# Attention with plain fp32 products in place of split ones, output by tokens, one PSUM pool, and the first two channel tiles interleaved

## The chip, the cores and the metric

The kernel runs on one core of a Trainium2 chip. A core has five engines with instruction streams of their own: TensorE (matmul and transpose, PE in the views, its weight loads PEld), VectorE (DVE), ScalarE (ACT), GpSimd (POOL) and SyncE (SP), which here issues most of the transfers. TensorE's results land in PSUM, eight banks of 128 x 512 fp32. The metric is the time of one execution in device microseconds; the times given are medians of several runs. One further execution was recorded by the hardware profiler. Its own time is given beside its span, since all rows below belong to it.

## The reference

One decoder layer over 512 tokens and 1024 channels, all in fp32: a SwiGLU FFN (inner width 2816), a mixing stage, a second FFN, each behind an RMSNorm and with a residual. The change is in the mixing stage:

```python
h = rms_norm(x, mix_norm_w[l])
z, xbc, dt_raw, q, k, v = jnp.split(h @ w_in[l], split_idx, axis=-1)
xbc = jax.nn.silu(causal_dwconv(xbc, conv_w[l], conv_b[l]))
...
y_ssd = ssd_chunked(xs, dt, a, bm, cm, d_skip[l])      # chunks of 128 tokens, 16 heads of 64
q = rms_norm(q.reshape(bsz, s, ATT_HEADS, 2, ATT_QK_DIM), q_norm_w[l])   # 8 heads, 2 halves of 64
k = rms_norm(k.reshape(bsz, s, ATT_HEADS, 2, ATT_QK_DIM), k_norm_w[l])
...
sc = jnp.einsum("bqhtd,bkhtd->bhtqk", qi, kf) * scale
p = jax.nn.softmax(jnp.where(mask, sc, -jnp.inf), axis=-1)
att = p[:, :, 0] - lam * p[:, :, 1]
o = jnp.einsum("bhqk,bkhd->bqhd", att, vf)             # v: 128 wide per head
o = rms_norm(o, attn_subln_w[l]) * (1.0 - lambda_init)
x = x + jnp.concatenate([y_ssd, o], axis=-1) @ w_out[l]
```

So each of 8 heads has two score matrices, and their softmaxes are subtracted before the product with v; the head's output is normed over its 128 channels.

## The kernel before, in words

Every large product is made of three matmuls in F32R, a single-pass type with fewer bits: an operand is split into a high part (the cast) and a low part (what the cast left), and hi·hi, hi·lo and lo·hi are summed in PSUM (`mm3`, L168 to L172; `tok_proj`, L590, with its matmuls in L603 to L605). Weights arrive by SyncE's transfers in pieces of 128 x 1024 (`raw`), `split_part` makes `whi` (ScalarE's cast in L128, or GpSimd in L126 while `pool_hi` is set) and `wlo` (VectorE's subtraction in L129). `piece()` asks for pieces two ahead. fp32 matmuls without a split exist beside them, such as cb (L644) and the transposes; the profile records a true fp32 product as two instructions.

The order within each engine is made by a scheduler from the program's text, with a simulated timeline; buffers and banks that come free, and true dependences, are its limits.

In time the stages are: FFN1 (0 to about 357 us), whose results are added to x by L362 channel tile by channel tile, each followed by the norm's scaling and split (`xh` L236, `xl` L237); the mixing stage; FFN2 (from about 843). The mixing stage is:

- Channel projections (L562 to L583): six pairs of 128-channel tiles, each tile 8 x 3 matmuls of 512 columns over `nm.xh`, `nm.xl`, weights stationary. `pA` gives two banks for a pair. The first pair also lets the norm finish (`finish`, L249: row sums into psr, the rsqrt chain of VectorE, psb). `conv_tile` (L470 to L488) does convolution and SiLU, `conv_tr` (L490) transposes by xt, `dt_proj` (L498 to L516) makes psdt and its transposes psdtT.
- SSD: z and v projections by tokens (`z_group`, `v_group`, L613 to L632) run between the chunks' work: `ssd_a` (L636: decay ab by Relu and Exp on ScalarE, its product with cb on VectorE, y), `ssd_o` and `ssd_d` (state, pd). v is stored split (`vhl`, L431).
- Attention (L966 to L998): the projections qk of heads 1 to 7 and parts of the head output wo serve as fillers (`fill`, L938) between the steps of a head. `qk_half` (L769) forms q and k and splits them (qs, kh, kl), `qk_tr` (L803) transposes them by 24 matmuls a head, `att_s` (L821) makes the scores of a 128-query block, masks, takes the maximum, the exponentials and the combination of the two softmaxes in pe; `att_t` (L848) transposes pe and splits it into atH and atL; `att_av` (L861) multiplies by v with channels on the partitions; `att_n` (L876) norms with a matmul with ones (om); `o_split` (L910) splits the result for wo. GpSimd takes part in nearly all of these.

PSUM is handed out by pools that are closed and opened again between stages (`psum_open`, L49): eight banks of one kind for FFN1, then A=2 (two banks each), M=2, J=2 (L424), then J=2, M=4, A=1 for attention, then eight again. A tile of a new pool waits for whoever reads the old pool's tile in the same place.

## Time and profile before

| what | value |
|---|---|
| median of 3 runs | 1196.5 us (1195.9 to 1197.11) |
| profiled execution | 1194.4 us, its span 1192.3 |
| mean granted TensorE clock | 0.992 |
| TensorE busy | 1160.0 us, 97% of the span |
| VectorE, ScalarE, GpSimd busy | 895.1, 569.6, 155.2 us |

The span is what the rows of the trace cover. A record's length is not the time that an instruction holds the engine: TensorE's records overlap by about 0.17 us, so the distance between two starts is the better measure. In the groups of instructions the part behind the bar gives the busy sum, the mean of one record in ns, and the idle time of the engine just before them with what ended it.

### The profile page before, as it was taken

Reading aid. Unit: us, or ns where it says so; the run is one execution under the profiler, and the core shown is the slowest. Engines: PE = TensorE matmul, PEld = TensorE weight load, DVE = VectorE, ACT = ScalarE, POOL = GpSimd, SP = SyncE. Lnnn points to the kernel's source line nnn. Section 1 sums busy time; section 2 is a strip of 40 time slices with the busy share of each in tenths; the row PEclk is TensorE's granted clock in tenths of the full one; section 3 lists DMA queues with packets and bytes.
Section 4 is the critical chain, followed back from the end, with each engine's and each line's share of the span. In section 5 each row is a group of like instructions: output and inputs, shape, how many; then the busy total and the mean of one; then the engine's idle time right before and its main releaser. Section 6 shows DMA issues by size and latency. Waiting matters only on the chain.

```text
span 1192.3 us, 18991 instructions
## 1 busy us (share of the span) xinstructions
PE 1160.0 (97%) x7483; PEld 1033.1 (87%) x7483; DVE 895.1 (75%) x1485; ACT 569.6 (48%) x991; POOL 155.2 (13%) x178
## 2 busy tenths in 40 slices
PE   8999999999998999999999998899999999999998
PEld 6889999999986788999988896688789999999997
DVE  6988787887675875976588988636599888787863
ACT  5433443343353448973366766735244444343331
POOL 1000000000022000000346656423000000000000
PEclk9999999999998999999999999999999999999999
DMA  6223333233253223423221103025213333333232
GB/s 231 89 76 98 100 108 99 92 111 106 89 186 127 77 90 107 142 89 110 88 70 48 60 19 124 27 63 211 80 62 105 108 111 98 110 107 102 96 108 84
DMA packets 42393, 119.56 MB, mean 100 GB/s; under 512 B 4608, under 2 KB 9920, under 8 KB 42304
## 3 DMA queue, kind: packets, MB, share of 16 engines
q1 hardware_dynamic: 41024, 114.15, 29.8%
q0 software_dynamic: 1280, 4.20, 1.0%
q8 instruction: 59, 0.97, 0.3%
q14 instruction: 30, 0.25, 0.1%
HBM read 112.00 MB, written 6.32 MB: 99 GB/s over the span
## 4 chain that ended last, share of the span: by engine, by line
PE 83%; DVE 8%; ACT 4%; issue 2%; POOL 1%; DMA 1%; SPq 0%; ACTq 0%; POOLq 0%; DVEq 0%
PE s L327 9%; PE s L326 9%; PE s L328 9%; PE dn L170 6%; PE dn L172 6%; PE dn L171 6%; PE gu L170 3%; PE gu L172 3%; PE gu L171 3%; PE wo L172 2%; PE wo L170 2%; PE wo L171 2%; PE xbc L170 2%; PE xbc L171 2%; PE xbc L172 2%
## 5 line engine op out<-in xcount | busy, mean ns | idle before, releaser
L128 ACT CAST whi<-raw 128x1024 fp32r<-128x1024 f32 (+2 forms) x204 | 176.6, 868 | 309.5 <-PE s L327 121.7
L129 DVE TENSOR_TENSOR wlo<-raw,whi 128x1024 fp32r<-128x1024 f32 (+3 forms) x225 | 226.5, 1010 | 113.4 <-ACT whi L128 102.0
L327 PE MATMUL s<-al,whi 128*128 128x256 f32 x952 | 265.0, 279 | 0.0
L326 PE MATMUL s<-ah,whi 128*128 128x256 f32 x952 | 263.4, 279 | 0.0
L328 PE MATMUL s<-ah,wlo 128*128 128x256 f32 x952 | 262.4, 279 | 0.0
L327 PEld LDWEIGHTS s<-al,whi 128*128 128x128 f32 x952 | 178.7, 188 | 2.1
L326 PEld LDWEIGHTS s<-ah,whi 128*128 128x128 f32 x952 | 178.3, 188 | 2.0
L328 PEld LDWEIGHTS s<-ah,wlo 128*128 128x128 f32 x952 | 177.1, 187 | 0.1
L128 ACT CAST whi<-tw 128x1024 fp32r<-128x1024 f32 x68 | 70.4, 1051 | 141.0 <-PE s L327 65.6
L170 PE MATMUL dn<-h,whi 128*128 128x512 f32 x352 | 137.5, 394 | 0.0
L172 PE MATMUL dn<-h,wlo 128*128 128x512 f32 x352 | 137.5, 392 | 0.0
L171 PE MATMUL dn<-h,whi 128*128 128x512 f32 x352 | 136.8, 389 | 0.0
L129 DVE TENSOR_TENSOR wlo<-tw,whi 128x1024 fp32r<-128x1024 f32 x68 | 82.0, 1220 | 2.9 <-ACT whi L128 2.8
L172 PEld LDWEIGHTS dn<-h,wlo 128*128 128x128 f32 x352 | 66.1, 188 | 14.6
L171 PEld LDWEIGHTS dn<-h,whi 128*128 128x128 f32 x352 | 66.1, 188 | 12.7
L170 PEld LDWEIGHTS dn<-h,whi 128*128 128x128 f32 x352 | 66.1, 188 | 12.2
L603 PE MATMUL qk<-whi,xhm 128*128 128x256 f32 x256 | 74.1, 289 | 0.3 <-DVE kf L781 0.3
L605 PE MATMUL qk<-whi,xlm 128*128 128x256 f32 x256 | 73.4, 287 | 0.0
L604 PE MATMUL qk<-wlo,xhm 128*128 128x256 f32 x256 | 73.1, 286 | 0.0
L362 DVE SCALAR_TENSOR_TENSOR x<-dn,x 128x512 f32<-128x512 f32 x64 | 44.1, 688 | 35.3 <-PE dn L172 34.8
L170 PE MATMUL gu<-xh,whi 128*128 128x512 f32 x160 | 65.0, 406 | 3.4 <-POOL whi L126 2.3
L172 PE MATMUL gu<-xh,wlo 128*128 128x512 f32 x160 | 63.7, 398 | 0.0
(293 smaller groups left out, 2529.1 us busy)
## 6 DMA issues: line engine op xcount, KB each, us to landing
raw<-in_gu SPq DMA_DIRECT2D x86, 512.0 KB, 3.5
raw<-in_dn SPq DMA_DIRECT2D x48, 384.0 KB, 3.1
raw<-in_wqk SPq DMA_DIRECT2D x16, 512.0 KB, 3.7
raw<-in_wxbc SPq DMA_DIRECT2D x12, 512.0 KB, 3.6
raw<-in_wo SPq DMA_DIRECT2D x10, 512.0 KB, 4.4
raw<-in_dn SPq DMA_DIRECT2D x16, 256.0 KB, 2.6
raw<-in_wz SPq DMA_DIRECT2D x8, 512.0 KB, 3.5
raw<-in_wv SPq DMA_DIRECT2D x8, 512.0 KB, 3.6
```

Of the source, the lines that this page charges most:

```text
L128: S.copy(hi[:, a:b], raw[:, a:b])
L129: V.tensor_sub(lo[:, a:b], raw[:, a:b], hi[:, a:b].bitcast(F32))
L170: PE.matmul(ps, lhsT=hi, rhs=xh, start=start, stop=False)
L171: PE.matmul(ps, lhsT=hi, rhs=xl, start=False, stop=False)
L172: PE.matmul(ps, lhsT=lo, rhs=xh, start=False, stop=stop)
L326: PE.matmul(ps, lhsT=hi, rhs=ah[:, i, a], start=i == 0, stop=False)
L327: PE.matmul(ps, lhsT=hi, rhs=al[:, i, a], start=False, stop=False)
L328: PE.matmul(ps, lhsT=lo, rhs=ah[:, i, a], start=False, stop=i == 3)
L362: V.scalar_tensor_tensor(x[d], ps, 0.5, x[d], op0=ALU.mult, op1=ALU.add)
L603: PE.matmul(o, lhsT=xh, rhs=hi, start=k == 0, stop=False)
L604: PE.matmul(o, lhsT=xh, rhs=lo, start=False, stop=False)
L605: PE.matmul(o, lhsT=xl, rhs=hi, start=False, stop=k == KD - 1)
```

## The change

PSUM becomes a single pool of eight one-bank tiles for the whole kernel; `pM`, `pJ` and `pP` are the same. In the first pair of channel tiles the loop over k is outside: for each k three matmuls of one tile and three of the other, into two banks; `finish` starts behind both, and the pair's convolution is issued behind the first tile of the second pair. v is kept in fp32 (`vt`).

In attention q and k stay fp32, 128 channels (both halves) to a row of tokens, so 8 fp32 transposes a head take the place of 24. The scores of half t use rows 64t to 64t+63 of the transposed q and k as a contraction over 64, one fp32 matmul for each half and query block, K columns long, into two banks. The combination of the softmaxes isn't divided by the first sum any more: pe0 − lam·(l0/l1)·pe1 is used, and the norm's epsilon is multiplied by l0² instead. The product with v is made by tokens: 10 fp32 matmuls of 128 x 128 a head; the norm is done there with a free-axis reduction, and `att_o` transposes the result (4 a head) and splits it. GpSimd has no part in it: weights' high parts and y's copy are ScalarE's. The order of steps in the loop over heads is changed. The diff, shortened:

```diff
--- before.py
+++ after.py
@@ -44,31 +44,12 @@
-    psum = {}
-    def psum_open(**bufs):
...
-    def pA(name):
-        return psum["A"][1].tile([P, 2, T], F32, tag="A", name=name)
+    pspool = ctx.enter_context(tc.tile_pool(name="psum", bufs=8, space=PSUM))
     def pM(name, dt=F32):
-        return psum["M"][1].tile([P, T], dt, tag="M", name=name)
-    def pJ(name):
-        return psum["J"][1].tile([P, T], F32, tag="J", name=name)
...
-    def pP(name):
-        return psum["P"][1].tile([P, T], F32, tag="P", name=name)
+        return pspool.tile([P, T], dt, tag="P", name=name)
+    pJ = pP = pM
...
@@ -421,16 +401,16 @@
-    psum_open(A=2, M=2, J=2)
...
-    vhl = [[mix.tile([P, NB, 256], F32R, tag=f"v{z}{g}", name=f"v{z}{g}") for z in "hl"] for g in range(4)]
+    vt = [mix.tile([P, NB, 256], F32, tag=f"v{g}", name=f"v{g}") for g in range(4)]
...
@@ -565,21 +545,30 @@
-        ps = pA(f"xbc{n}")
+        ps = [pP(f"xbc{n}{i}") for i in range(2)]
+        if n == 0:
+            ws = [piece(), piece()]
+            for k in range(KD):
+                for p_, w in zip(ps, ws):
+                    mm3(p_, w, k, nm.xh[:, k, :], nm.xl[:, k, :], k == 0, k == KD - 1)
+            fin = nm.finish()
+            next(fin)
+            first_ps = ps
+            continue
         for i in range(2):
             w = piece()
             for k in range(KD):
-                mm3(ps[:, i, :], w, k, nm.xh[:, k, :], nm.xl[:, k, :], k == 0, k == KD - 1)
-            if n == 0 and i == 0:
-                fin = nm.finish()
+                mm3(ps[i], w, k, nm.xh[:, k, :], nm.xl[:, k, :], k == 0, k == KD - 1)
+            if n == 1 and i == 0:
                 next(fin)
-            elif n == 0:
-                next(fin)
+                pend0 = [(t, conv_tile(t, p_)) for t, p_ in zip(order[0], first_ps)]
         if n == 3:
             dt_finish(pt_dt)
         for t, dst in pend:
             conv_tr(t, dst)
-        pend = [(t, conv_tile(t, ps[:, i, :])) for i, t in enumerate(pair)]
+        pend = [(t, conv_tile(t, ps[i])) for i, t in enumerate(pair)]
+        if n == 1:
+            pend = pend0 + pend
...
-                h, lo = (z[:, j, :] for z in vhl[g])
-                S.activation(h, ps[:, jj, :], AF.Copy, scale=nm.r[:, j:j + 1])
-                V.scalar_tensor_tensor(lo, ps[:, jj, :], nm.r[:, j:j + 1],
-                                       h.bitcast(F32), op0=ALU.mult, op1=ALU.subtract)
+                S.activation(vt[g][:, j, :], ps[:, jj, :], AF.Copy, scale=nm.r[:, j:j + 1])
...
@@ -667,11 +653,11 @@
-        pd = pds[c, g] = pA(f"pd{c}{g}")
+        pd = pds[c, g] = [pP(f"pd{c}{g}{i}") for i in range(2)[:2 if c else 1]]
         if c > 0:
-            PE.matmul(pd[:, 1, :], lhsT=cT[:, g, cs], rhs=state[:, g, :], start=True, stop=True)
+            PE.matmul(pd[1], lhsT=cT[:, g, cs], rhs=state[:, g, :], start=True, stop=True)
...
@@ -775,22 +761,12 @@
...
-        qf = at.tile([P, 2, P], F32, tag="qf", name="qf")
+        qf = at.tile([P, 2, P], F32, tag="qf", name="qf", bufs=4)
         V.tensor_tensor(qf, ps[:, :, 0:P], wqk_row.unsqueeze(1).to_broadcast([P, 2, P]), op=ALU.mult)
...
+        kf = at.tile([P, 2, P], F32, tag="kf", name="kf", bufs=4)
+        V.tensor_tensor(kf.rearrange("p a (b c) -> p a b c", c=64), ps[:, :, P:].rearrange("p a (b c) -> p a b c", c=64),
                         rs[:, :, 2:4].unsqueeze(3).to_broadcast([P, 2, 2, 64]), op=ALU.mult)
...
-        qk[h].append((rs, qs, kh, kl))
+        qk[h].append((rs, qf, kf))
     qk = {}
@@ -802,92 +778,91 @@
     def qk_tr(h):
         res = []
+        for si, tag in enumerate(("qT", "kT")):
+            pt = pM(f"{tag}{h}")
+            for j in range(NB):
+                PE.transpose(blk(pt, j), qk[h][j // 2][1 + si][:, j % 2, :], ident)
+            d = at.tile([P, T], F32, tag=tag, name=tag, bufs=2)
+            S.copy(d, pt)
+            res.append(d)
+        qkT[h] = res
+    ls, sm, aT = {}, {}, {}
+    def att_s(h, i):
+        K = (i + 1) * P
+        if i == 0:
+            ls[h] = tiny.tile([P, 2, NB], F32, tag="l", name="l", bufs=3)
+        ps = [pM(f"sc{h}{i}{t}") for t in range(2)]
+        qT, kT = qkT[h]
         for t in range(2):
...
-    def att_s(h, i):
-        K = (i + 1) * P
-        kc = max(K, 256)
...
+            r = slice(t * 64, t * 64 + 64)
+            PE.matmul(ps[t][:, :K], lhsT=qT[r, i * P:K], rhs=kT[r, :K], start=True, stop=False)
         for t in range(2):
-            qT, khT, klT = qkT[h][3 * t:3 * t + 3]
-            PE.matmul(ps[:, t, :kc], lhsT=blk(qT, i), rhs=khT[:, :kc], start=True, stop=False)
-            PE.matmul(ps[:, t, :kc], lhsT=blk(qT, i), rhs=klT[:, :kc], start=False, stop=False)
-            PE.matmul(ps[:, t, i * P:K], lhsT=identb, rhs=cmask, start=False, stop=True)
+            PE.matmul(ps[t][:, i * P:K], lhsT=identb, rhs=cmask, start=False, stop=True)
...
-        V.tensor_reduce(nmx, ps[:, :, :K], axis=AX, op=ALU.max, negate=True)
+        for t in range(2):
+            V.tensor_reduce(nmx[:, t:t + 1], ps[t][:, :K], axis=AX, op=ALU.max, negate=True)
         V.tensor_mul(nmx, nmx, rs[:, 0:2])
-        pe = at.tile([P, 2, T], F32, tag="pe", name="pe", bufs=3)
-        l = tiny.tile([P, 2], F32, tag="l", name="l")
+        pe = at.tile([P, 2, K], F32, tag=f"pe{i}", name="pe", bufs=2)
+        l = ls[h][:, :, i]
         for t in range(2):
-            S.activation(pe[:, t, :K], ps[:, t, :K], AF.Exp, bias=nmx[:, t:t + 1], scale=rs[:, t:t + 1],
+            S.activation(pe[:, t], ps[t][:, :K], AF.Exp, bias=nmx[:, t:t + 1], scale=rs[:, t:t + 1],
                          accum_out=l[:, t:t + 1])
...
-        G.tensor_scalar(pe[:, 0, :K], pe[:, 0, :K], l[:, 0:1], 1.0, op0=ALU.mult, op1=ALU.mult)
-        V.scalar_tensor_tensor(pe[:, 0, :K], pe[:, 1, :K], l[:, 1:2], pe[:, 0, :K], op0=ALU.mult, op1=ALU.add)
+        c = tiny.tile([P, 1], F32, tag="lc", name="lc")
+        V.reciprocal(c, l[:, 1:2])
+        V.scalar_tensor_tensor(c, l[:, 0:1], nlam[:, 0:1], c, op0=ALU.mult, op1=ALU.mult)
+        V.scalar_tensor_tensor(pe[:, 0], pe[:, 1], c[:, 0:1], pe[:, 0], op0=ALU.mult, op1=ALU.add)
         sm[h, i] = pe
     def att_t(h, i):
         K = (i + 1) * P
-        pe = sm[h, i]
+        pe = sm.pop((h, i))
         pt = pM(f"at{h}{i}")
         for kb in range(i + 1):
             PE.transpose(blk(pt, kb), pe[:, 0, kb * P:(kb + 1) * P], ident)
-        pv = pt[:, :K].rearrange("p (a b) -> p a b", b=P)
-        dh = atH[:, 0:i + 1, i * P:(i + 1) * P]
-        S.copy(dh, pv)
-        V.tensor_tensor(atL[:, 0:i + 1, i * P:(i + 1) * P], pv, dh.bitcast(F32), op=ALU.subtract)
-    osqs = {}
+        aT[h, i] = at.tile([P, K], F32, tag=f"aT{i}", name="aT", bufs=2)
+        S.copy(aT[h, i], pt[:, :K])
+    ons = {}
     def att_av(h):
         po = pM(f"o{h}")
-        vh, vl = (z[:, :, h % 2 * P:(h % 2 + 1) * P] for z in vhl[h // 2])
-        for kb in range(NB):
-            n0 = min(kb * P, 256)
-            st = dict(lhsT=vh[:, kb, :])
-            PE.matmul(po[:, n0:], rhs=atH[:, kb, n0:], start=kb == 0, stop=False, **st)
-            PE.matmul(po[:, n0:], rhs=atL[:, kb, n0:], start=False, stop=False, **st)
-            PE.matmul(po[:, n0:], lhsT=vl[:, kb, :], rhs=atH[:, kb, n0:], start=False,
-                      stop=kb == NB - 1)
...
+        for i in range(NB):
+            a = aT.pop((h, i))
+            for kb in range(i + 1):
+                PE.matmul(blk(po, i), lhsT=blk(a, kb), rhs=vt[h // 2][:, kb, h % 2 * P:(h % 2 + 1) * P],
+                          start=kb == 0, stop=kb == i)
+        oss = tiny.tile([P, NB], F32, tag="oss", name="oss")
+        osq = at.tile([P, NB, P], F32, tag="osq", name="osq")
+        S.activation(osq.rearrange("p a b -> p (a b)"), po, AF.Square)
+        V.tensor_reduce(oss, osq, axis=AX, op=ALU.add)
+        ov = tiny.tile([P, NB], F32, tag="ov", name="ov")
+        l0 = ls[h][:, 0, :]
+        V.scalar_tensor_tensor(ov, l0, EPS, l0, op0=ALU.mult, op1=ALU.mult)
+        V.scalar_tensor_tensor(ov, oss, 1.0 / 128, ov, op0=ALU.mult, op1=ALU.add)
+        orr = tiny.tile([P, NB], F32, tag="orr", name="orr")
+        rsqrt_act(orr, ov, [P, NB], "o")
+        on = ons[h] = at.tile([P, NB, P], F32, tag="on", name="on", bufs=2)
+        V.tensor_tensor(on, po.rearrange("p (a b) -> p a b", a=NB), orr.unsqueeze(2).to_broadcast([P, NB, P]), op=ALU.mult)
+    ohl = {}
+    def att_o(h):
+        g = h // 2
+        if g not in ohl:
+            ohl[g] = [mix.tile([P, 2, T], F32R, tag=f"{z}{g}", name=f"o{z}{g}") for z in ("v", "ol")]
+        pt = pM(f"oT{h}")
+        on = ons.pop(h)
+        for i in range(NB):
+            PE.transpose(blk(pt, i), on[:, i, :], ident)
+        oh, ol = (z[:, h % 2, :] for z in ohl[g])
+        S.activation(oh, pt, AF.Copy, scale=sub[:, 0:1])
+        V.scalar_tensor_tensor(ol, pt, sub[:, 0:1], oh.bitcast(F32), op0=ALU.mult, op1=ALU.subtract)
...
-            G.tensor_scalar(h, yt, 1.0, 1.0, op0=ALU.mult, op1=ALU.mult)
+            S.copy(h, yt)
             V.tensor_sub(yl[:, t:t + 2, :].rearrange("p a b -> p (a b)"), yt, h.bitcast(F32))
...
@@ -951,18 +916,11 @@
-    oT = at.tile([P, KD, T], F32, tag="oT", name="oT")
-    atH = at.tile([P, NB, T], F32R, name="atH")
-    atL = at.tile([P, NB, T], F32R, name="atL")
-    G.memset(atH[:, 3, 256:384].bitcast(F32), 0.0)
-    G.memset(atL[:, 3, 256:384].bitcast(F32), 0.0)
-    psum_open(J=2, M=4, A=1)
     fillers += [qk_proj(h) for h in range(1, 8)]
     fill()
     fill()
-    pool_hi[0] = True
     for h in range(8):
         qk_tr(h)
         fill()
@@ -971,26 +929,21 @@
             att_t(h - 1, 3)
         att_s(h, 0)
         att_s(h, 1)
-        if h > 0:
-            att_av(h - 1)
-            if h % 2 == 0:
-                o_split(h - 2)
         prep(taken[0] + 1)
         fill()
         if h == 6:
-            pool_hi[0] = False
             y_split()
             wo_ps[0], wo_ps[1] = pJ("wo0"), pJ("wo1")
             fillers += wo_fill(0)
-        att_t(h, 0)
+        if h > 0:
+            att_av(h - 1)
         att_s(h, 2)
-        if h > 0:
-            att_n(h - 1)
-            if h % 2 == 0:
-                o_split(h - 1)
         prep(taken[0] + 2)
         fill()
+        att_t(h, 0)
         att_t(h, 1)
+        if h > 1:
+            att_o(h - 2)
         att_s(h, 3)
         if h == 7:
             wo_ps[2], wo_ps[3] = pM("wo2"), pM("wo3")
@@ -1002,15 +955,16 @@
     att_t(7, 3)
     fill()
     att_av(7)
-    o_split(6)
+    att_o(6)
     fill()
...
```

The following fences show what this does to the engines' order, where L numbers of the second fence of a pair are those of the changed kernel. First, TensorE where FFN1 ends: dn is the last product of FFN1, xbc the first channel tiles. Before:

```order
L172 MATMUL dn_3_7_3450<-h,wlo 128x512
L170 MATMUL xbc_3517<-xhm,whi 128x512
L171 MATMUL xbc_3517<-xlm,whi 128x512
L172 MATMUL xbc_3517<-xhm,wlo 128x512
L170 MATMUL xbc_3517<-xhm,whi 128x512
L171 MATMUL xbc_3517<-xlm,whi 128x512
```

and now:

```order
L153 MATMUL dn_3_7_3450<-h,wlo 128x512
L151 MATMUL xbc_3504<-xhm,whi 128x512
L152 MATMUL xbc_3504<-xlm,whi 128x512
L153 MATMUL xbc_3504<-xhm,wlo 128x512
L151 MATMUL xbc_3505<-xhm,whi 128x512
L152 MATMUL xbc_3505<-xlm,whi 128x512
L151 MATMUL xbc_3504<-xhm,whi 128x512
L152 MATMUL xbc_3504<-xlm,whi 128x512
L153 MATMUL xbc_3505<-xhm,wlo 128x512
L153 MATMUL xbc_3504<-xhm,wlo 128x512
```

Two tiles, two tiles' weights and two banks now advance together through k. Second, TensorE at the scores of a fourth query block (sc, with qk a filler, at and oT transposes of attention). Before:

```order
L605 MATMUL qk_0_7039<-whi,xlm 128x256
L830 MATMUL sc_6748<-khT,qT 128x512
L831 MATMUL sc_6748<-klT,qT 128x512
L832 LDWEIGHTS identb
L832 MATMUL sc_6748<-cmask,identb 128x128
L830 MATMUL sc_6748<-khT,qT 128x512
L831 MATMUL sc_6748<-klT,qT 128x512
L832 LDWEIGHTS identb
L832 MATMUL sc_6748<-cmask,identb 128x128
L603 MATMUL qk_0_7039<-whi,xhm 128x256
```

and now:

```order
L825 MATMUL at_6557<-ident,pe 128x128 x2
L862 MATMUL oT_6564<-ident,on 128x128 x4
L801 MATMUL sc_6571<-kT,qT 128x512
L801 MATMUL sc_6572<-kT,qT 128x512
L803 LDWEIGHTS identb
L803 MATMUL sc_6571<-cmask,identb 128x128
L803 LDWEIGHTS identb
L803 MATMUL sc_6572<-cmask,identb 128x128
L594 MATMUL qk_0_6528<-whi,xlm 128x256
```

The products of both halves follow each other directly, and the masks come behind both. Third, ScalarE from the last z products to the Exp of ab, which the first pd of the SSD needs (y is the D·x product, ab the decay, th and sz belong to z). Before:

```order
L660 ACTIVATE y<-xs,row 128x64 x8
L128 CAST whi<-raw 128x1024
L660 ACTIVATE y<-xs,row 128x64 x2
L128 CAST whi<-raw 128x1024
L660 ACTIVATE y<-xs,row 128x64 x2
L619 ACTIVATE th<-z_1_4277,hr 128x256
L648 ACTIVATE ab<-ab,acs 128x128 x8
L620 ACTIVATE sz<-z_1_4277,hr 128x256
L619 ACTIVATE th<-z_1_4277,hr 128x256
L620 ACTIVATE sz<-z_1_4277,hr 128x256
L681 COPY state<-st_4335 128x512
L648 ACTIVATE ab<-ab,acs 128x128 x8
```

and now:

```order
L646 ACTIVATE y<-xs,row 128x64 x15
L634 ACTIVATE ab<-ab,acs 128x128 x8
L109 CAST whi<-raw 128x1024
L634 ACTIVATE ab<-ab,acs 128x128 x3
L608 ACTIVATE th<-z_1_4270,hr 128x256
L609 ACTIVATE sz<-z_1_4270,hr 128x256
L608 ACTIVATE th<-z_1_4270,hr 128x256
L609 ACTIVATE sz<-z_1_4270,hr 128x256
L667 COPY state<-st_4328 128x512
L109 CAST whi<-raw 128x1024
L634 ACTIVATE ab<-ab,acs 128x128 x3
L635 ACT_TABLE_LOAD
```

The products are the same in kind; most y products stand together ahead of ab, and the second group's ab products are spread around the weights' casts.

## Rows read from the trace of the kernel before

**Rows 1.** Page, part 1: busy us (share of span) x instructions, by engine.
```profile
PE 1160.0 (97%) x7483; PEld 1033.1 (87%) x7483; DVE 895.1 (75%) x1485; ACT 569.6 (48%) x991; POOL 155.2 (13%) x178
```
**Rows 2.** Windows: stretch, length, each engine busy (x instructions), PE clock, DMA share, GB/s.
```profile
450.00:480.00 30.00, 28.09 (x226) 25.95 (x225) 17.14 (x27) 27.90 (x73) 0.00 (x0) 1.00 0.35 115
580.00:850.00 270.00, 252.52 (x1622) 217.12 (x1621) 193.75 (x379) 156.31 (x365) 131.18 (x125) 0.99 0.24 79
580.00:590.00 10.00, 7.80 (x61) 7.66 (x60) 6.99 (x18) 5.16 (x14) 4.56 (x4) 0.83 0.30 105
```
**Rows 3.** Groups of TensorE: operation, count, busy us, mean ns, idle before and releasers.
```profile
L830 PE MATMUL sc<-khT,qT 128*128 128x256 f32 (+2 forms) x64 | 25.1, 393 | 2.2 <-ACT pe L840 1.5 <-ACT khT L815 0.6
L831 PE MATMUL sc<-klT,qT 128*128 128x256 f32 (+2 forms) x64 | 20.6, 326 | 0.0
L832 PE MATMUL sc<-cmask,identb 128*128 128x128 bf16 x64 | 14.7, 230 | 0.0
L853 PE MATMUL at<-ident,pe 128*128 128x128 f32 x80 | 14.6, 280 | 8.2 <-DVE pe L845 3.5 <-DVE l L843 2.6 <-ACT atH L856 1.2
L868 PE MATMUL o<-atL,vh 128*128 128x256 f32 (+2 forms) x32 | 10.5, 327 | 0.1
L879 PE MATMUL om<-osq,ones 128*128 128x512 f32 x16 | 8.3, 601 | 0.0
L810 PE MATMUL qT<-identr,qs 128*128 128x128 f32 x64 | 8.1, 248 | 2.2 <-POOL qs L789 2.2
L171 PE MATMUL wo<-yl,whi 128*128 128x512 f32 x64 | 26.3, 411 | 2.7 <-DVE yl L903 2.7
```
**Rows 4.** Timeline of TensorE around psdtT: start us, us, engine, line, operation.
```profile
409.87 0.40 PE L170 MATMUL xbc<-xhm,whi 128*128 128x512 f32 x1
410.19 0.45 PE L515 MATMUL psdtT<-ident,dtr 48*128 48x48 f32 x4
...
410.91 0.40 PE L172 MATMUL xbc<-xhm,wlo 128*128 128x512 f32 x1
411.14 0.39 PE L170 MATMUL xbc<-xhm,whi 128*128 128x512 f32 x1
```
**Rows 5.** Timeline of TensorE where FFN1 ends; in brackets the idle before.
```profile
363.11 0.76 PE L170 MATMUL xbc<-xhm,whi 128*128 128x512 f32 x1 [5.57 <-DVE x L362]
363.67 0.63 PE L171 MATMUL xbc<-xlm,whi 128*128 128x512 f32 x1
```
**Rows 6.** Timeline of VectorE from the end of FFN1 to the norm's end.
```profile
362.29 0.68 DVE L362 SCALAR_TENSOR_TENSOR x<-dn,x 128x512 f32<-128x512 f32 x1
...
364.02 1.76 DVE L237 SCALAR_TENSOR_TENSOR xlm<-x,col,xhm 128x512 fp32r<-128x512 f32 x1
...
375.45 0.15 DVE L255 TENSOR_SCALAR vm<-psrm 128x4 f32<-128x4 f32 x1
...
377.90 0.69 DVE L262 TENSOR_TENSOR accm<-ident,rm 128x512 f32<-128x512 f32 x1
```
**Rows 7.** The tile psdt: who reads it, ns min/median/max.
```profile
L512 ACT COPY dtr<-psdt x1: 582/582/582, 405.2 to 405.2; 48x512 f32<-48x512 f32 x1
```
**Rows 8.** Timeline of TensorE in the SSD: the last xt and the first pd.
```profile
452.02 0.60 PE L494 MATMUL xt<-ident,xst 128*128 128x128 f32 x4
...
470.05 2.00 PE L690 MATMUL pd<-xdt,ab 128*128 128x64 f32 x16 [0.77 <-DVE ab L653]
```
**Rows 9.** Timeline of ScalarE in the same stretch: the first y and the Exp.
```profile
454.58 2.04 ACT L660 ACTIVATE y<-xs,row 128x64 f32<-128x64 f32 x8
...
467.68 1.07 ACT L649 ACTIVATE ab<-ab 128x1024 f32<-128x1024 f32 x1
```
**Rows 10.** Groups of TensorE: an fp32 product, and the token projections of z.
```profile
L644 PE MATMUL cb<-cT,bT 128*128 128x128 f32 x16 | 3.1, 276 | 0.0
L604 PE MATMUL z<-wlo,xhm 128*128 128x256 f32 x128 | 35.6, 278 | 0.0
```
**Rows 11.** Groups of GpSimd between 580 and 850: the weights' high parts.
```profile
L126 POOL TENSOR_SCALAR whi<-raw 128x1024 fp32r<-128x1024 f32 x11 | 14.0, 1275 | 0.4 <-PE qk L605 0.4
```

97 lines of the change are left out of this document (16 added, 81 removed).

## The prediction

> **What bounds the kernel now.** I read the busy times of the page first: TensorE is busy 1160.0 of 1192.3 us, 97%, the next engine 75% [rows 1]. So time is saved in two ways only: TensorE gets less to do, or its 32 us of idleness shrink. Next I read windows of those stretches that the diff touches, to see how much of the idleness is theirs. Around attention and head output (580 to 850) TensorE is idle 270 − 252.5 = 17.5 us; in 450 to 480 it is idle 1.9 us while ScalarE is busy 27.9 of 30, so there ScalarE is near to being the bound [rows 2]. At the boundary behind the first FFN one gap of 5.57 us stands in TensorE's timeline [rows 5]. These 25 us are what the change can reach; both FFNs keep their code.
>
> Then I read TensorE's groups [rows 3]. A record's duration there is not what an instruction costs: records overlap. Two neighbours start 411.14 − 410.91 = 0.23 us apart while each is recorded with 0.40 [rows 4]. So I take a mean less 0.165 as the slot of an instruction (0.40 − 0.23 within the two digits of the rows). This is an estimate, made from 512-column rows and used for all sizes.
>
> **The change part by part.** The forecast is a sum against the profiled execution, 1194.4 us (span 1192.3 and 2.1 around it); the median of the runs, 1196.5, lies 2.1 above that, and 2.1 is added at the end.
>
> *FFN1 to mix.* Today the pools of banks are reopened, so the first xbc matmul waits for the last reader of the old banks, the add of x7, which ends at 362.29 + 0.68 = 362.97; TensorE starts at 363.11. It then runs at the lower of its two clocks, 1.2 GHz: 13 records of 0.63 like the second row follow instead of 0.40, 0.2 us more each, 2.5 us [rows 5, 6]. With one pool two banks are free at 357.5, and the slices of xn for k up to 5 are there or come in time (k = 7 ends at 364.02 + 1.76 = 365.78 [rows 6]). Interleaving gives 6 matmuls, 6 × 0.23 = 1.4 us, for each k, so k = 7 is wanted at 357.5 + 7 × 1.4 = 367.3 and is there 1.5 us early. The gap and the slow clock go: −8.1. Two new waits come. The matmuls of psb now stand right behind the 24 of the next tile, and the chain of VectorE that feeds them takes 375.45 to 378.59, 3.1 us, with weight splits ahead of it [rows 6]: I take 1.2. The transposes psdtT, today 22 matmuls behind psdt, follow directly and wait for the copy of 0.58 us, behind silus on ScalarE [rows 7]: I take 0.9. Both could be nothing or twice that. Sum −6.1 (−8.1 to −4).
>
> *SSD.* Splitting pA into single banks costs nothing by itself. But in the new order the first pd comes sooner: between the last xt and it stand 96 matmuls of tok_proj, one st and two cb, 96 × 0.113 + 0.87 + 4 × 0.111 = 12.2 us [rows 3, 10], where today TensorE has work for nearly the whole stretch from the last xt, 452.02 + 0.60 less the overlap, 452.4, to pd at 470.05, 17.7 us [rows 8]. What ScalarE must do in that stretch, from the D·x products at 454.58 to the Exp of ab that ends at 467.68 + 1.07 [rows 9], is the same list in another order, two more products of one kind and two fewer of the other. So pd would wait up to 17.7 − 12.2 = 5.5 us, and nothing if ScalarE is further on by then; I take 4.0, nearer the upper end since its list is the same. That is about as long as the gap at the boundary, so I let the clock fall behind it too, at 1.6, less than the 2.5 there. The matmuls that stood ahead of pd come later and fill part of today's 1.9 us of idleness, all of which I count as given back: 4.0 + 1.6 − 1.9 = +3.7 (−2 to +7).
>
> *Waits in attention.* Today's 17.5 us fall on qT waiting for GpSimd's qs (2.2), at for the combination of the softmax and the split tiles (8.2), wo for yl (2.7), sc for banks and for khT (2.2) and smaller ones [rows 3]. qs is gone. The combination loses the GpSimd step, and its transposes stand behind one more filler. Each query block has its own aT, and eight banks of one kind take the place of three kinds. What stays: a wait of 1 for kT at the first head, 3 where head 7 has few fillers, 2 for yl (whose copy moves to ScalarE), 1 for banks, 2 for the rest: 9. That is −8.3 (−13 to 0). The clock also fell in two stretches, 580 to 590 (0.83 granted, while TensorE was busy 7.80 of 10) and 760 to 770, which reads 0.83 as well [rows 2]; 0.17 × 10 is 1.7 us each at most, 3.1 taken for both: −3.1. The cover for all this is ScalarE and VectorE, busy 156 and 194 of 270. What moves from GpSimd to ScalarE is the weights' high part, 11 copies of 1.275 us there [rows 11], and four copies of y; the long norm activations of ScalarE and VectorE's splits go. Both stay well under TensorE, and I cost it at nothing; if I am wrong, fillers come late, and that is the rival of replaced waits.
>
> *TensorE's work.* Slots today, from [rows 3]: scores 64 × 0.228 + 64 × 0.161 + 64 × 0.065 = 29.1; o 96 × 0.16 = 15.3 (three alike lines of 32); om 16 × 0.436 = 7.0; 192 transposes qT, khT, klT × 0.08 = 15.4. Together 66.8. Afterwards: 96 transposes like at, 280 − 165 ns, 11.0; masks 4.2 as now; o by tokens 80 fp32 products of two records, 160 × 0.111 (cb [rows 10]) = 17.8. The 80 transposes at and all F32R projections stay. The scores are new in kind: 64 fp32 products on 64 rows, two records each, of 128 to 512 columns. With 0.111 for 128 columns (cb) and 0.436 for 512 (om), one head has four records of each size, 4 × (0.111 + 0.218 + 0.327 + 0.436) = 4.37, all 34.9 if everything runs one after the other; half of that, 17.5, if the two halves of the array run together. I take three quarters, 26.2: the products come in the order of the program, half 0 with both passes, then half 1, so only the second pass of one can lie over the first of the other. No row shows products on the two halves; both ends are kept.
>
> There is a price for changing from 128 rows to fewer, and one row has it: psdtT on 48 rows. From the start of the matmul ahead at 409.87 to that of the second behind, 410.91, 1.04 us pass [rows 4]; two matmuls take 0.46 and four tiny transposes at most 0.25, so some 0.33 is left over. The scores go in and out 32 times: 32 × 0.325 = 10.4 (0 to twice that).
>
> The Trainium skill says the same in kind: its page "TensorEngine Tiling (Array Packing)", section Key Properties, has a change of the tiling mode drain TensorE. The row bears that out with its third of a microsecond; the rule gives no price, so with it alone the sum would be 10.4 lower.
>
> Sum 11.0 + 4.2 + 17.8 + 26.2 + 10.4 = 69.6 against 66.8: +2.8 (−16 with full overlap and no price, +11.5 with no overlap and the price).
>
> All: −6.1 + 3.7 − 8.3 − 3.1 + 2.8 = −11.0. The profiled execution would be 1183.4, the median 1185.5; **1185**.
>
> **The rivals.** *The halves don't overlap.* For it: every other pair of products in the trace goes in order on the whole array. The scores then cost 8.7 more: 1194.
> *The halves overlap fully.* 8.7 less: 1176. It wants both passes of one half to lie beside both of the other. The Trainium skill's page "TensorEngine Tiling (Array Packing)", section Theoretical Speedup, gives up to 2x for contractions of at most 64. No row shows it, and the order within the halves speaks against it here, so its chance is small.
> *The halves drain the array between them (slower).* If the step from half 0 to half 1 within a block is paid like that into and out of 48 rows, there are 32 more such prices on top of serial halves: 8.7 + 10.4 = 19.1, 1204. The change is slower from (1198.9 − 1194) / 32 = 0.15 us for each step on. For it: psdtT's leftover. Against: there the number of rows changed, here only which rows.
> *Waits are only replaced.* The combination of the softmax keeps its chain of reduce, two exponentials, reciprocal and product; if TensorE stands there as long as now, the 8.3 are not won: 1193.
>
> **How the numbers follow.** Forecast 0.42, serial halves 0.20, full overlap 0.15, replaced waits 0.12, drained halves 0.11. The smallest difference that can be told is about 0.2%: faster ends at 1194.1, slower begins at 1198.9. The forecast and full overlap lie on the faster side whole (0.56 with a little left over); serial halves and replaced waits, at 1194 and 1193, give half of theirs to faster (0.17), a good third to same (0.12), the rest (0.05) to slower; drained halves go to slower but for a fifth. That makes 0.73, 0.13, 0.14. The range goes from 1171, under full overlap with its own uncertainty of 5, to 1199, over serial halves and a few us of other misses; some 0.1 lies above, under drained halves, and 0.05 below.
>
> **What would show it.** At the boundary: first xbc right behind the last dn, no record of 0.63 there. In 580 to 850 (or what it becomes): idle near 9, the clock at 1.00, GpSimd almost still. For the scores: distance from a block's first score matmul to its mask: for 512 columns 4 × 0.436 = 1.74 if serial, 1.31 by the forecast, 0.87 with full overlap; what is beyond is the price of the switch. At the first pd: a wait of about 4 us put down to ab. It is wrong if TensorE's records in attention sum to another figure than above by more than 8 us, or if the SSD stage, which I saw in the order alone, runs later than today by more than 6.

## The result, and the profile after

The changed kernel takes 1178.66 us (median of 4 runs, 1177.35 to 1180.52) against 1196.2 of the kernel before on the same chip: ratio 0.986 with a 95% interval of 0.9847 to 0.9872, so 17.5 us less. The forecast was 1185 in a range of 1171 to 1199. The profiled execution has a span of 1177.2 us. The first line of the page answers to [rows 1]:

```profile
PE 1163.6 (99%) x7435; PEld 1026.4 (87%) x7435; DVE 854.4 (73%) x1509; ACT 546.0 (46%) x938; POOL 36.0 (3%) x63
```

TensorE is busy 99% of the span instead of 97%, and for 3.6 us *longer* than before, although the change takes work from it. Both are taken up below: the idleness under the waits in attention, the longer work under the addresses. Windows of the changed kernel, to be read beside [rows 2] (the attention is some 20 us shorter, so the long window is too):

```profile
460.00:470.00 10.00, 6.18 (x31) 6.18 (x32) 5.51 (x8) 8.97 (x20) 0.00 (x0) 0.72 0.32 105
580.00:830.00 250.00, 248.79 (x1602) 206.93 (x1601) 163.58 (x426) 133.54 (x314) 15.55 (x15) 0.99 0.27 84
740.00:755.00 15.00, 13.79 (x46) 8.23 (x45) 7.60 (x23) 5.53 (x17) 0.00 (x0) 0.77 0.00 0
```

Around attention TensorE is idle 250 − 248.8 = 1.2 us, where it was 17.5. GpSimd is nearly still. Two stretches have a low granted clock: one in the SSD (0.72) and one at the end of attention (0.77).

The boundary behind FFN1, on TensorE, answers to [rows 5]:

```profile
361.14 0.40 PE L152 MATMUL dn<-h,whi 128*128 128x512 f32 x1
361.38 0.40 PE L153 MATMUL dn<-h,wlo 128*128 128x512 f32 x1
361.61 0.40 PE L151 MATMUL xbc<-xhm,whi 128*128 128x512 f32 x1
```

The first xbc follows the last dn without a gap, and its record has 0.40, not 0.63. Of the two new waits of that stage psb's doesn't show, and psdtT's is 0.67 us:

```profile
390.26 0.45 PE L495 MATMUL psdtT<-ident,dtr 48*128 48x48 f32 x4 [0.67 <-ACT dtr L492]
```

The SSD's first pd, with what ScalarE did ahead of it, answers to [rows 8, 9]:

```profile
463.82 3.21 PE L676 MATMUL pd<-xdt,ab 128*128 128x64 f32 x16 [4.69 <-DVE ab L639]
```
```profile
448.54 3.69 ACT L646 ACTIVATE y<-xs,row 128x64 f32<-128x64 f32 x15
...
461.45 1.06 ACT L635 ACTIVATE ab<-ab 128x1024 f32<-128x1024 f32 x1
```

ScalarE spends 3.69 us on D·x products before it comes to ab, whose Exp ends at 462.51. TensorE waits 4.69 us and then runs pd in 3.21 us, where it took 2.00 before.

The scores, on TensorE (start, us, form; x4 is two products of two records each), the first block with the two transposes of pe ahead of it, and that block's weight loads:

```profile
600.28 0.38 PE L825 MATMUL at<-ident,pe 128*128 128x128 f32 x2
600.59 1.13 PE L801 MATMUL sc<-kT,qT 64*128 64x512 f32 x4
601.65 0.28 PE L803 MATMUL sc<-cmask,identb 128*128 128x128 bf16 x2
...
609.14 0.49 PE L801 MATMUL sc<-kT,qT 64*128 64x128 f32 x4
609.57 0.29 PE L803 MATMUL sc<-cmask,identb 128*128 128x128 bf16 x2
609.78 0.70 PE L801 MATMUL sc<-kT,qT 64*128 64x256 f32 x4
610.42 0.28 PE L803 MATMUL sc<-cmask,identb 128*128 128x128 bf16 x2
...
612.03 0.91 PE L801 MATMUL sc<-kT,qT 64*128 64x384 f32 x2
612.87 0.23 PE L803 MATMUL sc<-cmask,identb 128*128 128x128 bf16 x1
...
633.35 0.92 PE L801 MATMUL sc<-kT,qT 64*128 64x384 f32 x4
634.20 0.29 PE L803 MATMUL sc<-cmask,identb 128*128 128x128 bf16 x2
```
```profile
600.59 0.30 PEld L801 LDWEIGHTS sc<-kT,qT 64*128 64x128 f32 x4 [0.17 <-issue]
```

From the first score to the mask it is 1.06, 0.43, 0.64 and 0.85 us for 512, 128, 256 and 384 columns. The block at 612.03 has one half alone (x2), since the scheduler put other work between the halves of head 1's third block: it takes 0.84 us, as long as both halves together at 633.35. So two halves that follow each other run in the time of one. Three more blocks, one of head 6 and two of head 7, have their halves apart, with one half's mask between them. The weight load of a block starts together with its matmul, not ahead of it.

### The profile page after: what moved, and what is told of

It reads as the page before. It is cut to its first block, busy times and chain, and to the rows that moved or that the text cites. A ratio compares the mean times of both kernels' runs of the same rounds, so it can differ in the third digit from the quotient of the medians.

```text
span 1177.2 us, 18641 instructions
## 1 busy us (share of the span) xinstructions
PE 1163.6 (99%) x7435; PEld 1026.4 (87%) x7435; DVE 854.4 (73%) x1509; ACT 546.0 (46%) x938; POOL 36.0 (3%) x63
## 4 chain that ended last, share of the span: by engine, by line
PE 97%; ACT 1%; DMA 0%; DVE 0%; SPq 0%; issue 0%; POOL 0%
PE s L308 10%; PE s L306 10%; PE s L307 10%; PE dn L153 7%; PE dn L152 7%; PE dn L151 7%; PE gu L151 3%; PE gu L152 3%; PE gu L153 3%; PE qk L592 3%; PE wo L151 3%; PE wo L152 3%; PE wo L153 3%; PE qk L594 3%; PE qk L593 3%; PE sc L801 2%
## 5 line engine op out<-in xcount | busy, mean ns | idle before, releaser
L109 ACT CAST whi<-raw 128x1024 fp32r<-128x1024 f32 (+2 forms) x217 | 189.5, 875 | 316.9 <-PE s L307 123.1
L110 DVE TENSOR_TENSOR wlo<-raw,whi 128x1024 fp32r<-128x1024 f32 (+3 forms) x225 | 223.0, 993 | 127.6 <-ACT whi L109 121.7
L152 PE MATMUL gu<-xl,whi 128*128 128x512 f32 x160 | 63.6, 398 | 0.0
```

Source lines behind the costliest of these rows:

```text
L109: S.copy(hi[:, a:b], raw[:, a:b])
L110: V.tensor_sub(lo[:, a:b], raw[:, a:b], hi[:, a:b].bitcast(F32))
L152: PE.matmul(ps, lhsT=hi, rhs=xl, start=False, stop=False)
```

## The experiments

All times are medians. The kernel before took 1195.4 to 1195.9 us beside them.

### The two kernels once more, on one chip

> The kernel before, unchanged, profiled once more. In the two profiles at hand a 512-column F32R matmul of the FFNs starts every 0.229 us in the kernel before and every 0.233 us in the changed one, 6.7 us over both FFNs, although their code is the same. If that belongs to the execution or the chip, this profile and the next show one slot for both kernels; if it belongs to the kernel, this one shows 0.229 again and the next 0.233.

> The changed kernel, unchanged, profiled beside the one before. Ratio again 0.986. The mixing stage from the last dn to the first gu of the second FFN 22 us shorter, whatever the FFNs' slots are; first pd waits 4 to 5 us and two stretches of 6.8 us at 1.2 GHz.

The changed kernel gave 1178.11 us, ratio 0.9856 (0.9834 to 0.9879); the kernel before 1198.37 in its one run. TensorE's stages in the two profiles of this pair, from start to start of the instructions named; the last starts are 19.9 us apart:

| stage (TensorE) | before | after | difference | forecast |
|---|---|---|---|---|
| to the last dn of FFN1 | 357.1 | 359.5 | +2.4 | 0 |
| last dn to first xbc | 5.9 | 0.2 | −5.7 | −6.1, with the clock behind it |
| first xbc to last pd | 186.1 | 190.5 | +4.4 | +3.7 |
| last pd to first qT | 32.5 | 32.8 | +0.3 | 0 |
| first qT to first gu of FFN2 | 266.0 | 242.1 | −23.9 | −8.6 |
| first gu to the end | 344.7 | 347.3 | +2.6 | 0 |

The mixing stage, from the last dn to the first gu, is 24.9 us shorter, where 22 was expected from the first pair of profiles (22.0 there); the wait at the first pd is 4.70 us, and the stretches at 1.2 GHz are 6.8 and 10.2 us long, not 6.8 each. This pair's kernel before has four stretches of 3.4 us at 1.2 GHz in attention, the first pair's has two.

The FFNs, whose code is the same, are 5 us slower; in the first pair of profiles it is 4.3 and 2.6, together 6.9. (Here only the kernel before has a stretch at 1.2 GHz at its start: the clock from 0 to 20 us is 0.91 in it and 1.00 in the changed kernel.) A stretch of dn matmuls of FFN1 in either kernel, first and last row, no other instruction between:

```profile
344.56 0.39 PE L171 MATMUL dn<-h,whi 128*128 128x512 f32 x1
...
346.84 0.39 PE L172 MATMUL dn<-h,wlo 128*128 128x512 f32 x1
```
```profile
344.81 0.40 PE L153 MATMUL dn<-h,wlo 128*128 128x512 f32 x1
...
346.91 0.40 PE L152 MATMUL dn<-h,whi 128*128 128x512 f32 x1
```

Before, 10 steps take 2.28 us, 0.228 each; after, 9 take 2.10, 0.233. The profiles of this pair show the same two slots, 0.229 and 0.233. So it belongs to the kernel, and not to the execution.

### Tile after tile at the boundary

> One pool of banks stays, but the first pair of channel tiles runs tile after tile, so the slice k = 7 of xn is wanted 21 matmuls, 4.9 us, behind the last dn instead of 42. In the kernel before that slice was ready 8.2 us behind it. Theory: a wait of about 3.4 us comes back at the boundary, with a stretch at 1.2 GHz behind it: +3.4 to +6.8. Rival: the pool alone had removed the gap: no change within 1 us.

```diff
-            for k in range(KD):
-                for p_, w in zip(ps, ws):
+            for p_, w in zip(ps, ws):
+                for k in range(KD):
                     mm3(p_, w, k, nm.xh[:, k, :], nm.xl[:, k, :], k == 0, k == KD - 1)
```

1179.68 us, ratio 0.987 (0.9837 to 0.9903), the same as the changed kernel. The rival holds. TensorE at the boundary:

```profile
359.45 0.40 PE L153 MATMUL dn<-h,wlo 128*128 128x512 f32 x1
359.69 0.40 PE L151 MATMUL xbc<-xhm,whi 128*128 128x512 f32 x1
```

There is no gap, and no wait over 0.1 us follows in the pair: where a slice of xn is late, the scheduler takes matmuls of the second tile. The single pool removed the 5.57 us; the loop written in another order is worth nothing measurable.

### Halves one after the other

> Half 0, its mask, half 1, its mask, in every block, so the halves never run together. Theory from the trace of the changed kernel, where four blocks stand so by themselves and one half alone takes 0.84 us for 384 columns, as long as both together: 28 blocks lose their overlap, 0.424 + 0.635 + 0.848 + 1.062 a head, 23.75 for 8 heads less 3.8 of the four blocks: +20 us, about 1199. Rival, the forecast's own three quarters: a half alone costs two thirds of a pair, +6.7 us, about 1185.

```diff
         for t in range(2):
             r = slice(t * 64, t * 64 + 64)
-            PE.matmul(ps[t][:, :K], lhsT=qT[r, i * P:K], rhs=kT[r, :K], start=True, stop=False)
-        for t in range(2):
-            PE.matmul(ps[t][:, i * P:K], lhsT=identb, rhs=cmask, start=False, stop=True)
+            mm = PE.matmul(ps[t][:, :K], lhsT=qT[r, i * P:K], rhs=kT[r, :K], start=True, stop=False)
+            if t:
+                behind(mm, m0)      # issue order only
+            m0 = PE.matmul(ps[t][:, i * P:K], lhsT=identb, rhs=cmask, start=False, stop=True)
```

1197.79 us, ratio to the kernel before 1.0014 (1.0003 to 1.0026): 19.7 us slower than the changed kernel, as the first theory has it (+20), and three times the rival (+6.7). A block of 512 columns:

```profile
602.56 1.12 PE L805 MATMUL sc<-kT,qT 64*128 64x512 f32 x2
603.62 0.23 PE L808 MATMUL sc<-cmask,identb 128*128 128x128 bf16 x1
603.77 1.12 PE L805 MATMUL sc<-kT,qT 64*128 64x512 f32 x2
604.83 0.23 PE L808 MATMUL sc<-cmask,identb 128*128 128x128 bf16 x1
```

Each half takes 1.06 us, as both did together. The sum came out partly by luck: by the starts the scores and their masks take 21 us more than in the changed kernel, and some 3 come back elsewhere, since this profile has neither the wait nor the stretch at 1.2 GHz at the end of attention. With products on 64 rows the whole gain of the change hangs on the two halves' standing side by side; the next run shows that the gain can be had without such products.

### Scores on all 128 rows

> The scores contract over all 128 rows, with kT copied into two tiles whose other half is zero: no 64-row products at all. Theory (the halves overlap fully and a 64-row pass costs only 0.1 us more than its columns): the scores take 34.9 us by the slots of 0.111 to 0.436, against about 27.5 now: +7, about 1186. Rival, the forecast's term (going to 64 rows costs 0.325 a block, three quarters overlap, 36.6 together): 2 us less than that, so the time would fall by 2.

```diff
# kT is copied into two tiles, one per half, whose other 64 rows are zero
...
-            PE.matmul(ps[t][:, :K], lhsT=qT[r, i * P:K], rhs=kT[r, :K], start=True, stop=False)
+            PE.matmul(ps[t][:, :K], lhsT=blk(qT, i), rhs=kT[t][:, :K], start=True, stop=False)
```

1179.42 us, ratio 0.9864 (0.9844 to 0.9883): 1.3 above the changed kernel, neither +7 nor −2. The blocks have the length that the first theory gives them, with no price at either end:

```profile
600.34 0.39 PE L831 MATMUL at<-ident,pe 128*128 128x128 f32 x2
600.46 0.30 PEld L807 LDWEIGHTS sc<-kz,qT 128*128 128x128 f32 x2
600.56 1.88 PE L807 MATMUL sc<-kz,qT 128*128 128x512 f32 x4
602.28 0.28 PE L809 MATMUL sc<-cmask,identb 128*128 128x128 bf16 x2
```

1.72 us is 4 × 0.43, against 1.06 on 64 rows. Part of what the time gives back stands in the window of the end of attention:

```profile
740.00:755.00 15.00, 13.55 (x76) 10.30 (x75) 10.11 (x33) 7.53 (x23) 0.00 (x0) 1.00 0.15 51
```

The clock is 1.00 there, where the changed kernel has 0.77: 0.23 × 15 = 3.5 us. By the distances of starts the scores take 35.2 us against 28.9 (of which 1.4 in the slow clock), +6.3; the masks behind them 3.0 against 4.5, the transposes of pe and the products with v 1.5 less together, wo 1.9 less. That makes +1.4, as measured. What comes back is in about equal parts the clock and the way into a 64-row block: the two transposes ahead of the block take 0.22 us here (600.34 to 600.56) and 0.31 in the changed kernel (600.28 to 600.59), and the same 0.09 is missing behind a product with v (0.111 us to the first score against 0.205) and behind a mask (0.056 against 0.151). TensorE waits 1.45 us in that window, and 1.21 us in the changed kernel's, so the longer wait is the one without a fall of the clock. Why isn't settled by these runs. So 128 rows with zeros come out like the 64-row halves here, but 3.4 us of that are the slow stretch, which the last run below is rid of with 64 rows too.

### The D·x products behind the Exp

> In the SSD the eight D*x products of a step are issued behind that step's Exp of ab on ScalarE instead of ahead of it. Theory: the first pd waits only because ScalarE does 15 of them, 3.69 us, and gates of z ahead of the Exp: the wait of 4.69 us goes below 1 us and so does the stretch of 6.8 us at 1.2 GHz behind it (3.4 us lost): -7 to -8. Rival: the wait moves to the next pd or to y, since ScalarE has the same work to do: within 2 us.

```diff
-        S.activation(ab, ab, AF.Exp, scale=-1.0)
+        ex = S.activation(ab, ab, AF.Exp, scale=-1.0)
...
-            S.activation(y[:, h, :], xg[:, h, :], AF.Copy, scale=row[...])
+            yi = S.activation(y[:, h, :], xg[:, h, :], AF.Copy, scale=row[...])
+            behind(yi, ex)          # issue order only
```

1170.19 us, ratio 0.9789 (0.9761 to 0.9818): 8 us less than the changed kernel, as the theory has it. ScalarE, TensorE and the window:

```profile
455.15 1.06 ACT L635 ACTIVATE ab<-ab 128x1024 f32<-128x1024 f32 x1
456.11 2.01 ACT L646 ACTIVATE y<-xs,row 128x64 f32<-128x64 f32 x8
```
```profile
457.52 2.00 PE L678 MATMUL pd<-xdt,ab 128*128 128x64 f32 x16 [0.71 <-DVE ab L639]
```
```profile
455.00:465.00 10.00, 9.29 (x70) 8.13 (x69) 7.05 (x10) 9.99 (x29) 0.00 (x0) 1.00 0.41 139
```

The wait is 0.71 instead of 4.69, and the clock stays at 1.00. The 4 us and the 6.8 us at 1.2 GHz behind it, half of which was lost, make 7.4. No later pd waits for it, although ScalarE is as full as before.

### The order of steps, and GpSimd's casts

> The steps of a head in the order of the kernel before (product with v ahead of the second filler, first transposes ahead of the third scores), with everything else of the changed kernel. Theory: GpSimd's absence and the one pool removed most of TensorE's idle time in attention, 16 us: idle stays under 4, +1 to +3. Rival: the order removed it: idle is back at 8 or more, +7 or more.

> The weights' high parts are made by GpSimd again during attention, 11 to 12 casts of 1.3 us in place of ScalarE's 0.88, nothing else. Theory: TensorE's fillers are supplied early enough either way, no change within 1.5 us. Rival: GpSimd's slower casts and its sharing with VectorE delay wlo, and idle of several us comes back: +3 or more.

```diff
# the old order of steps: in the loop over heads
         att_s(h, 1)
+        if h > 0:
+            att_av(h - 1)
         prep(taken[0] + 1)
...
-        if h > 0:
-            att_av(h - 1)
+        att_t(h, 0)
         att_s(h, 2)
+        if h > 1:
+            att_o(h - 2)
         prep(taken[0] + 2)
         fill()
-        att_t(h, 0)
         att_t(h, 1)
-        if h > 1:
-            att_o(h - 2)
```
```diff
# GpSimd's casts: ahead of the loop over heads, and at its seventh head
+    pool_hi[0] = True
...
+            pool_hi[0] = False
```

1180.85 us (0.9876, 0.9848 to 0.9904) and 1181.96 us (0.989, 0.986 to 0.992): 2 to 4 us slower, the first hardly more than the scatter. TensorE's groups of the transposes of pe with the old order, and of the scores with the casts on GpSimd and in the changed kernel:

```profile
L825 PE MATMUL at<-ident,pe 128*128 128x128 f32 x80 | 14.0, 273 | 2.3 <-DVE pe L817 2.3
```
```profile
L801 PE MATMUL sc<-kT,qT 64*128 64x128 f32 (+3 forms) x128 | 35.6, 489 | 0.0
```
```profile
L801 PE MATMUL sc<-kT,qT 64*128 64x128 f32 (+3 forms) x128 | 31.3, 493 | 0.0
...
L825 PE MATMUL at<-ident,pe 128*128 128x128 f32 x80 | 13.8, 272 | 1.2 <-DVE nmx L808 1.2
```

Neither brings the idleness back: 2.3 us, as the theory has it, and with the casts 1.2 as in the changed kernel. In the old order six blocks have their halves apart instead of four. What the casts cost is of another kind than either theory had: the scores take 4.3 us more, because the scheduler put other work between the halves in 9 blocks of 32 instead of 4. So the 16 us of idleness that went are not due to the order of steps nor to the weights' casts. What is left are GpSimd's part in the softmax and in the splits, the split copies themselves, and the pools; these weren't tried apart.

### Addresses

> The changed kernel with 32 bytes more in the pool of constants and in the small tiles' pool, so that weights and moving operands lie at the addresses modulo 64 that they had in the kernel before (the new tile nlam had pushed the weights on by 32 bytes); every engine's order is the same. In the profiles a 512-column F32R matmul starts every 0.229 us where both operands are at 0 modulo 64, and every 0.233 us where one is at 0 and the other at 32 (all of the changed kernel but the gate and up products of FFN2; the same products of FFN2 in the kernel before). Theory: the addresses make the slot; 2016 such matmuls gain 4.1 ns, 192 lose 6.5: -7, about 1171. Rival: the slot comes from something else of the change: no difference within 1.5 us.

> Only the small tiles' pool is 32 bytes longer: weights stay at 32 modulo 64 and the moving operands go there too, as in the products of FFN2's gate and up in the changed kernel, which start every 0.2267 us. Theory: operands that lie alike modulo 64 are read without the delay, and 32 is as good as 0 or better: 2016 matmuls gain 4 to 6.5 ns: -8 to -13, 1165 to 1170. Rival: the 0.2267 belongs to those products and not to the address: no difference, or the time of the run with both at 0.

```diff
# both; the second kernel has the second line only
+    const.tile([P, 8], F32, name="padc")                      # behind nlam
+    tiny.tile([P, 8], F32, tag="padt", name="padt", bufs=1)   # first tile of the small tiles' pool
```

1179.22 us (0.9857, 0.9833 to 0.9881) and 1177.35 us (0.9837, 0.9817 to 0.9857): no gain that can be told. In the trace the theory is right for 512 columns all the same, and fails for 256. With both at 0, dn in FFN1 (13 steps), and s, the products of 256 columns (11 steps):

```profile
342.78 0.39 PE L153 MATMUL dn<-h,wlo 128*128 128x512 f32 x1
...
345.72 0.62 PE L153 MATMUL dn<-h,wlo 128*128 128x512 f32 x2
```
```profile
149.77 0.28 PE L307 MATMUL s<-ah,whi 128*128 128x256 f32 x1
...
151.09 0.28 PE L309 MATMUL s<-ah,wlo 128*128 128x256 f32 x1
```

2.94 / 13 = 0.226 us against 0.233, but 1.32 / 11 = 0.120 us against 0.118 in the changed kernel, here over 21 steps:

```profile
149.78 0.28 PE L307 MATMUL s<-al,whi 128*128 128x256 f32 x1
...
152.26 0.28 PE L307 MATMUL s<-al,whi 128*128 128x256 f32 x1
```

The second kernel has the same two slots. So it isn't the address modulo 64 but the distance between the moving operand and the weights: the two kernels place weights and moving operands 32 bytes apart and leave that distance as it is. Only for gate and up of FFN2 does it differ between them, −32 and 0, and there the slot does too, 0.233 and 0.227. The mean times between starts, over whole stages of the four profiles, ordered by that distance (moving operand less weights, from the addresses that the pools give out, modulo 256 bytes):

| distance | 512 columns | 256 columns (s) | seen in |
|---|---|---|---|
| 0 | 0.227 to 0.228 | 0.120 | both pads, without gate and up of FFN2 in the first; gate and up of FFN2 in the changed kernel |
| 64 | 0.229 | 0.118 | kernel before |
| 32 either way | 0.233 | 0.118 | changed kernel; gate and up of FFN2 in the kernel before |

At −64, where the pads put the attention's share of wo, 512 columns take 0.233 to 0.234. By these slots the 512-column products gain 9 to 10 us with the pads and the 4392 of 256 columns (s and the token projections) lose 8, which fits the two times.

It also shows that nlam isn't the cause. Like the pad behind it, it pushes the weights and nearly all that lies behind them by the same 32 bytes. What moved the distance from 64 to −32 is the small tiles' pool, which lies between the weights and the moving operands: it has 13 buffers of 32 bytes more in the changed kernel, for the new small tiles of the softmax and the norm.

> The changed kernel with the D*x products behind the Exp of ab, as in the run that gave 1170.2, and with pads that choose where moving operands lie against the weights, modulo 256 bytes. The profiles so far give for a distance of 0 / 64 / 32 bytes a slot of 0.2268 / 0.2292 / 0.2333 us for 512 columns and 0.1200 / 0.1176 / 0.1182 for 256. Here h, the operands of FFN2's gate and up and the attention's share of wo are at 0, the operands of the seven-product FFN part and of the projections by tokens at 64. Theory: 512 columns gain 1056 x 6.5 ns + 768 x 4.1 + 192 x 6.5, 256 columns 2856 x 0.6: -13, about 1157.5. Rival: what one length of product gains is lost elsewhere, as in the two runs with pads before: 1170 again, within 2 us.

```diff
# with the D·x products behind the Exp
+    tiny.tile([P, 24], F32, tag="padt", name="padt", bufs=1)
...
         sp, hp = sp_cm.__enter__(), hp_cm.__enter__()
+        hp.tile([P, 48], F32, tag="padh", name="padh", bufs=1)
```

1158.4 us, ratio 0.9685 (0.9652 to 0.9719), where 1157.5 was expected: 12 us below the run with the D·x products alone, for two tiles that nobody reads.

### The halves tied

> As the run beside it, and in the four blocks whose two score halves stand apart in the changed kernel (heads 1, 6, 7 and 7) the halves are kept in program order, which puts three of the four together. Theory: each such block saves the time of one half, 0.84, 1.06 and 1.06 us: -3 us against the run beside it. Rival: the half that is ready first waits for its partner's bank, and TensorE stands for as long: within 1 us.

```diff
+        tied = (h, i) in ((1, 2), (6, 3), (7, 2), (7, 3))
         for t in range(2):
...
+            if tied:
+                tc.keep_in_program_order(mm)
...                                   # half 0's mask likewise
```

1152.29 us, ratio 0.9641 (0.9626 to 0.9655), 6 us below the run beside it, twice what was expected. The last block of the last head, then the wait ahead of it and the window of the end of attention:

```profile
725.96 1.22 PE L806 MATMUL sc<-kT,qT 64*128 64x512 f32 x4
727.11 0.28 PE L810 MATMUL sc<-cmask,identb 128*128 128x128 bf16 x2
```
```profile
725.18 0.41 PE L834 MATMUL at<-ident,pe 128*128 128x128 f32 x2 [0.57 <-DVE pe L826]
725.00:740.00 15.00, 14.62 (x72) 11.43 (x73) 9.02 (x23) 7.30 (x16) 0.00 (x0) 1.00 0.08 21
```

and the same wait and window in the run beside it:

```profile
726.65 0.41 PE L829 MATMUL at<-ident,pe 128*128 128x128 f32 x2 [1.21 <-DVE nmx L812]
725.00:740.00 15.00, 13.79 (x48) 9.16 (x48) 6.82 (x22) 5.78 (x15) 0.00 (x0) 0.77 0.00 0
```

Three blocks have both halves side by side again (3 us). With the scores of the last blocks complete sooner the wait of 1.21 us became one of 0.57, and the stretch at 1.2 GHz behind it, 6.8 us in the run beside it, of which half is lost, is gone too. This is the fastest version; it beats both kernels, the changed one by 26 us.

## Why the prediction was right, and where its terms were not

The direction, the range and the main places were right; of the terms only the first two were sized well. The number is near by luck in part: the waits in attention and TensorE's work were taken 18 us too long together, and 9 us went the other way (the FFNs, the clock's 3.1 that didn't come, a little in the SSD).

*FFN1 to mix* (−6.1): the gap and the slow clock went, as worked out, and psdtT waits 0.67 us for the taken 0.9. psb's wait of 1.2 us doesn't show. But the step that gave the interleaving its part was wrong: with one pool, tile after tile costs nothing (the run on the boundary). The scheduler interleaves by itself where a slice is late, which I hadn't looked for.

*SSD* (+3.7): 4.69 us of wait for the taken 4.0, and a clock loss of 3.4 for 1.6; from first xbc to last pd, 4.4 us with what the boundary's clock gave back. The mechanism was right, as the run with the products behind the Exp shows; it also was avoidable, which the forecast didn't ask.

*Waits in attention* (−8.3): the mis-sized step is "what stays: … 9" (and 17.5 − 9 is 8.5, not 8.3). 1.2 us stay. Each of the waits that I kept (kT, head 7, yl, banks) vanished. The runs on the order and on the casts exclude two reasons; which of the others did it is open. The clock's −3.1 didn't come: the stretches at 580 and 760 went, and others came, in the SSD and at 744, behind a wait of 1.21 us.

*TensorE's work* (+2.8): by the starts in the pair of profiles the kinds that change took 69.9 us before (66.8 by the forecast's slots) and 62.9 after (69.6): −7. The step that failed is the overlap in the scores, three quarters of 34.9, 26.2. "Only the second pass of one can lie over the first of the other" is wrong: both passes of half 0 run beside both of half 1, so four records last as long as two. The price of 0.325 a block, read from psdtT, was about right, but lies elsewhere: a block of 512 columns takes 1.06, where two passes of 0.436 make 0.87, so 0.19 is left in the block, some 0.1 for each pass, and 0.09 is paid on the way in, 0.28 together. The weight loads, which start with their matmul there instead of ahead of it, have that size (0.30 us recorded for four that run in pairs). On 128 rows the first one starts 0.10 us ahead of its matmul, and a block has nothing left over. That fits, but no run took the loads away. The Trainium skill's page "TensorEngine Tiling (Array Packing)", section Theoretical Speedup, with up to 2x for contractions of 64, is what the trace shows: 0.85 for both halves and 0.84 for one. Its section Key Properties, with the drain at a change of mode, fits the 0.09 us on the way in. The 0.1 us between two passes of a block, where the mode stays, is as long.

*What the sum left out* is that the FFNs don't keep their time: +5 to +7 us, because the new small tiles shift the moving operands against the weights. It hid a part of the gain: the mixing stage alone is 22.0 to 24.9 us shorter in the two pairs of profiles, against −11.0.

So the rival "full overlap" (1176) was the true case of the scores. The forecast's 1185 lay near the result because an overlap that was taken too small, idleness that was kept too large and a loss that was not foreseen partly cancel. The changed products are 6.7 us off their sum, where 8 was to show the mechanism wrong, and the SSD runs 4.4 later, where 6 was.

## What to carry to other kernels

Two contractions over 64 rows should be issued back to back on different row halves and banks, and the order that comes out should be looked at block by block: a filler between them, be it one mask, costs the whole of one half. Zeros on the other 64 rows ask for no such order; they cost 1.3 us more here, some 5 without the slow stretch that only the halves had. Where an engine waits for another that is full, look at what that engine does ahead of the awaited result and isn't wanted yet. When kernels whose hot loops are the same differ by a per cent all over, compare the time between two starts in the same loop, and then the distance between the operands' addresses.
